# A 16-piece, 64-byte DRAM-to-DRAM copy at the head of ScalarE's DMA queue, in a softmax with relative-position bias

## The chip, the cores and the metric

The kernel runs on one core of a Trainium2 (trn2) chip; nothing else runs on the chip's other cores as far as this case tells. The metric is device time in microseconds, the median of several executions. The profile comes from one execution of its own, whose time stands beside its span below.

## The reference

For each of 2 x 8 (batch, head) pairs there is a 2112 x 2112 matrix of float32 logits. A bias that depends only on the clipped distance between row and column is added, and a softmax is taken along each row:

```python
B, H, S = (2, 8, 2112)
max_rel = 16
rel = pos[:, None] - pos[None, :]
rel_clipped = np.clip(rel, -max_rel, max_rel) + max_rel
bias = rel_bias[:, rel_clipped].copy()          # rel_bias: (H, 33)
logits = logits + bias[None, :, :, :]
logits = logits - logits.max(axis=-1, keepdims=True)
exp = np.exp(logits)
return (exp / exp.sum(axis=-1, keepdims=True)).astype(np.float32)
```

Input and output are 285.5 MB each, and both must cross between DRAM and the on-chip memory once.

## The kernel before

The 2 x 8 x 2112 rows are one long list, cut into 128 equal runs of ROWS = 264 rows, one run for each partition. So 8 neighbouring partitions (PB = 8) hold one (batch, head) matrix, and there are 16 such groups. A tile takes R = 6 rows of every partition: 128 x 12672 float32, 6.49 MB (6336 KB). There are N = 44 tiles, and NBUF = 4 buffers X[0] to X[3] through which they turn in place.

For each tile: SyncE's queue (SP) loads it (`load`, L80). VectorE (DVE) takes each of the six rows, adds the bias from a strip F and forms the negated row maximum (`add`, L187). ScalarE (ACT) takes exp with the row sum (`exps`, L196). DVE forms reciprocals of three rows at a time and scales the rows (`scale`, L204 and L208). ScalarE's queue stores the tile to the output (`store`, L84) once six rows are scaled. SP issues the load into a buffer again when the buffer's store has landed (the loop at L229). Everything is ordered by hand with semaphores: `take` waits for a count and takes it off again.

What comes ahead of the first tile matters here. SP issues load 0 at once, then a small load of 15 pieces of 10,240 bytes into the last buffer (L110, 150 KB; load 3 overwrites it later), then loads 1 and 2, and load 3 when the small one has landed. ScalarE's queue waits until DVE has cleared 264 columns of F (L99), then loads rel_bias into F, one row of 1,056 bytes for each of the 16 groups (L102). DVE waits for that (L143), turns it into the long bias line M in PSUM (L143 to L176), copies a strip of M into F (L181), and starts on tile 0 (L187). ScalarE's next work after L102 is the exp of tile 0, with its table load (L196), and its next DMA is the first store (L84).

The last tile's store is issued in two halves. At the end SP waits for both.

Of the kernel before, what the change touches and what calls it, by code (L numbers as in the profile page):

```python
# [15 lines left out]
def kernel(  # L16
# [6 lines left out]
    nc = tc.nc  # L23
    P = 128
    B, H, S, S2 = logits.shape
# [3 lines left out]
    ROWS = B * H * S // P  # L29
    PB = S // ROWS  # L30
# [8 lines left out]
    FW = S + STEP - 1  # L39
    BIG = 3.0e38  # L40
    LOW, PAD = 32, 2560

    io = ctx.enter_context(tc.tile_pool(name="io", bufs=1))
    X = [io.tile([P, R * S], FP32, tag=f"X{b}", name=f"X{b}") for b in range(NBUF)]
# [9 lines left out]
    def view(t, offset, dims):  # L54

        return bass.AP(tensor=t.tensor, offset=t.offset + offset, ap=[[list(t.ap[0])[0], P]] + dims)

    def rows(t, j, n):

        return bass.AP(tensor=t.tensor, offset=t.offset + j * S, ap=[[ROWS * S, P], [1, n * S]])  # L60

    with tc.tile_critical(no_gpsimd_drain=True):  # L62
# [7 lines left out]
        idx = nc.alloc_semaphore("idx")  # L70
        dve = nc.alloc_semaphore("dve")
        even = nc.alloc_semaphore("even")
        landed = tc.alloc_semaphore("landed")

        def take(eng, sem, n):
            eng.wait_ge(sem, n).then_inc(sem, -n)  # L76


        def load(j, b):
            nc.sync.dma_start(out=X[b][:, :], in_=rows(logits, j, R)).then_inc(ld[b], 16)  # L80
# [11 lines left out]
        def then(ins):  # L92
            done[0] += 1
            ins.then_inc(dve, 1)

        def settle():
            v.wait_ge(dve, done[0])

        then(v.memset(F[:, 0 : H * W], 0.0))  # L99

        nc.scalar.wait_ge(dve, 1)
        nc.scalar.dma_start(  # L102
            out=bass.AP(tensor=F.tensor, offset=F.offset, ap=[[PB * list(F.ap[0])[0], P // PB], [1, H * W]]),
            in_=bass.AP(
                tensor=rel_bias.tensor, offset=rel_bias.offset, ap=[[0, P // PB], [1, H * W]]
            ),
        ).then_inc(rb, 16)
        load(0, 0)
        pad = X[NBUF - 1]
        nc.sync.dma_start(  # L110
            out=bass.AP(tensor=pad.tensor, offset=pad.offset + LOW * list(pad.ap[0])[0],
                        ap=[[4 * list(pad.ap[0])[0], 15], [1, PAD]]),
            in_=bass.AP(tensor=logits.tensor, offset=logits.offset + (LOW * ROWS + (NBUF - 1) * R) * S,
                        ap=[[4 * ROWS * S, 15], [1, PAD]]),
# [24 lines left out]
        for m, op in ((eq, ALU.is_equal), (gt, ALU.is_gt), (le, ALU.is_le), (lt, ALU.is_lt)):  # L139
# [4 lines left out]
            out=view(F, 0, [[W, H], [1, W]]), in0=view(F, 0, [[W, H], [1, W]]),  # L144
# [8 lines left out]
                           in_=view(F, RT, [[Q, 2], [PB, Q // PB], [0, PB]])))  # L153
# [9 lines left out]
            out=view(F, 0, [[W, PB], [1, W]]), in0=view(F, SC + 2 * PB, [[1, PB], [0, W]]),  # L163
# [7 lines left out]
            out=view(M, U, [[ROWS, PB], [1, W]]), in0=view(F, 0, [[W, PB], [1, W]]),  # L171
            in1=view(F, SC + 8 * PB, [[1, PB], [0, W]]), op=ALU.add))
        then(v.tensor_copy(out=view(M, U + W, [[ROWS, PB], [1, ROWS - W]]),  # L173
                           in_=view(F, SC + 7 * PB, [[1, PB], [0, ROWS - W]])))
# [91 lines left out]
```

## Time and profile before

| what | value |
|---|---|
| device time, median of 3 runs | 1328.96 us (1327.49 to 1329.62) |
| the profiled execution's own time | 1327.58 us |
| its span, first to last instruction | 1325.7 us |
| bytes moved by DMA in the span | 571.14 MB, mean 431 GB/s |
| VectorE busy | 977.9 us, 74% |
| ScalarE busy | 574.3 us, 43% |
| loads of a tile | 44, median 40.9 us from issue to landing |
| stores of a tile | 43 whole and 2 halves, median 56.4 us for a whole one |

The profiled execution lies 1.38 us under the median, inside the range of the three runs, and 1.88 us of its time lie outside the span. In the DMA part of the page, q1 is the queue that SP issues to and q10 is ScalarE's; q14 fetches instructions. A queue's share is the time that its packets took as a share of 16 DMA engines for the stretch asked about. A packet counts in the window in which it starts, so a share can come out a little over 1. A tile's DMA is 128 packets of 50,688 bytes, 8 on each of the 16 DMA engines, and one 4-byte semaphore packet on each engine. "DVEq" and "ACTq" stand for the engine's own instruction queue: a wait put down to line L76 (`take`) is a wait for a semaphore that was taken there, on DVE in `add` for a load, on ACT in `exps` for a row from DVE.

### The profile page before, as it was taken

The page shows a single profiled execution, that of the slowest core. Times are in us where ns is not written, and L with a number is a line of the kernel's source. Part 1 is how long each engine was busy: PE and PEld are TensorE (multiplying, and loading weights), DVE is VectorE, ACT ScalarE, POOL GpSimd, SP SyncE. Part 2 cuts the span into 40 slices and gives each one's busy share as a digit, 9 for nine tenths or more (in the row PEclk, how much of TensorE's full clock was granted, in tenths as well). Part 3 has the DMA queues.
Part 4 walks back from the last instruction along what each step waited for, and adds up shares of the span by engine and source line. Part 5 has one row for each costly group of instructions (what it writes and reads, how often), then busy time and mean ns, then how long its engine had stood idle before and what let it go on. Part 6 is the DMA issues. An engine that isn't in the chain of part 4 may idle for free. (4 is left out here: it accounts for less than half of the span.)

```text
span 1325.7 us, 2475 instructions
## 1 busy us (share of the span) xinstructions
DVE 977.9 (74%) x917; ACT 574.3 (43%) x538; POOL 0.4 (0%) x6
## 2 busy tenths in 40 slices
DVE  7998777667877787677778777766877787676774
ACT  3464333434444443334444443433444443333442
POOL 0000000000000000000000000000000000000000
DMA  9999999999999999999999999999999999999998
GB/s 409 419 425 440 437 424 434 440 436 422 437 439 436 425 436 439 428 430 439 440 424 433 440 437 424 436 440 431 428 437 440 425 431 440 439 422 436 439 436 355
DMA packets 12880, 571.14 MB, mean 431 GB/s; under 512 B 1455, under 2 KB 1471, under 8 KB 1471
## 3 DMA queue, kind: packets, MB, share of 16 engines
q1 hardware_dynamic: 6366, 285.63, 49.9%
q10 hardware_dynamic: 6512, 285.49, 49.8%
q14 instruction: 2, 0.02, 0.0%
HBM read 285.65 MB, written 285.47 MB: 431 GB/s over the span
## 5 line engine op out<-in xcount | busy, mean ns | idle before, releaser
L187 DVE CUSTOM_DVE_ANT_0 X<-X,F 128x2112 f32<-128x2112 f32 x264 | 605.2, 2355 | 307.5 <-DVEq L76 307.5
L196 ACT ACTIVATE X<-X,nmax 128x2112 f32<-128x2112 f32 x264 | 541.7, 2052 | 558.4 <-ACTq L76 538.3
L208 DVE TENSOR_SCALAR X<-X,rec 128x2112 f32<-128x2112 f32 x264 | 332.5, 1316 | 13.2
L196 ACT ACT_TABLE_LOAD x10 | 12.8, 1283 | 169.0 <-ACTq L76 169.0
L196 ACT ACTIVATION_READ_ACCUMULATOR X<-X,nmax 128x1 f32 x264 | 49.2, 186 | 0.0
L181 DVE COPY F<-M 128x2135 f32 x11 | 26.1, 2375 | 0.5 <-DVEq L210 0.5
L187 DVE DVE_READ_ACCUMULATOR2_ANT nmax<- 128x1 f32 x264 | 22.0, 83 | 0.0
L204 DVE RECIPROCAL rec<-tot 128x3 f32<-128x3 f32 x88 | 15.0, 171 | 0.0
L143 DVE TENSOR_TENSOR F<-F 128x264 f32<-128x264 f32 x1 | 0.4, 434 | 7.0 <-DMA F<-in_rel_bias_dram 7.0
L173 DVE COPY M<-F 128x1848 f32<-128x1848 f32 x1 | 2.1, 2079 | 0.0
L99 DVE MEMSET F<- 128x264 f32 x1 | 0.3, 278 | 1.1 <-SPq L62 1.1
L147 DVE TENSOR_REDUCE F<-F 128x33 f32<-128x264 f32 x1 | 0.6, 611 | 0.0
L170 DVE TENSOR_TENSOR M<-F 128x264 f32<-128x264 f32 x1 | 0.4, 442 | 0.0
L162 DVE TENSOR_TENSOR F<-F,rbS 128x264 f32<-128x264 f32 x1 | 0.4, 427 | 0.0
L140 DVE TENSOR_SCALAR F<-F 128x8 f32<-128x8 f32 x4 | 0.4, 168 | 0.0
L175 DVE COPY M<-rbS 128x247 f32<-128x247 f32 x1 | 0.4, 408 | 0.0
L150 DVE STREAM_TRANSPOSE F<-F 128x64 f32<-128x64 f32 x1 | 0.2, 245 | 0.0
L155 DVE STREAM_TRANSPOSE F<-F 128x64 f32<-128x64 f32 x1 | 0.2, 245 | 0.0
L160 DVE TENSOR_SCALAR F<-F,rbS 128x8 f32<-128x8 f32 x1 | 0.2, 231 | 0.0
L166 DVE SCALAR_TENSOR_TENSOR F<-F,rbS 128x8 f32<-128x8 f32 x1 | 0.2, 229 | 0.0
L161 DVE TENSOR_SCALAR F<-F,rbS 128x8 f32<-128x8 f32 x1 | 0.2, 225 | 0.0
L167 DVE SCALAR_TENSOR_TENSOR F<-F,rbS 128x8 f32<-128x8 f32 x1 | 0.2, 222 | 0.0
(15 smaller groups left out, 2.1 us busy)
## 6 DMA issues: line engine op xcount, KB each, us to landing
X<-in_logits_dram SPq DMA_DIRECT2D x44, 6336.0 KB, 40.9
out_dram<-X ACTq DMA_DIRECT2D x43, 6336.0 KB, 56.4
out_dram<-X ACTq DMA_DIRECT2D x2, 3168.0 KB, 15.5
X<-in_logits_dram SPq DMA_DIRECT2D x1, 150.0 KB, 17.5
F<-in_rel_bias_dram ACTq DMA_DIRECT2D x1, 16.5 KB, 8.1
```

The source lines that it names most:

```text
L140: then(v.tensor_scalar(out=m, in0=dp, scalar1=0.0, scalar2=None, op0=op))
L143: then(v.tensor_tensor(out=view(F, 0, [[W, H], [1, W]]), in0=view(F, 0, [[W, H], [1, W]]), in1=view(F, SC + 3 * PB, [[1, H], [0, W]]), op= ...
L147: then(v.tensor_reduce(out=F[:, RB : RB + W], in_=view(F, 0, [[1, W], [W, H]]), axis=mybir.AxisListType.X, op=ALU.add))
L162: then(v.tensor_tensor(out=view(F, 0, [[W, PB], [1, W]]), in0=view(F, SC + 2 * PB, [[1, PB], [0, W]]), in1=view(rbS, W - 1, [[0, PB], [-1, ...
L170: then(v.tensor_tensor(out=view(M, U, [[ROWS, PB], [1, W]]), in0=view(F, 0, [[W, PB], [1, W]]), in1=view(F, SC + 8 * PB, [[1, PB], [0, W]] ...
L173: then(v.tensor_copy(out=view(M, U + W, [[ROWS, PB], [1, ROWS - W]]), in_=view(F, SC + 7 * PB, [[1, PB], [0, ROWS - W]])))
L175: then(v.tensor_copy(out=M[:, 0:U], in_=low.to_broadcast([P, U])))
L181: v.tensor_copy(out=F[:, :], in_=M[:, bass.ds(ROWS - STEP - j, FW)]).then_inc(dve, 1)
L187: v.tensor_tensor_reduce(out=x, in0=x, in1=F[:, STEP - 1 - r : STEP - 1 - r + S], scale=-1.0, scalar=BIG, op0=ALU.add, op1=ALU.min, accum_ ...
L196: nc.scalar.activation(out=x, in_=x, func=EXP, scale=-1.0, bias=nmax[:, r : r + 1], accum_out=tot[:, r : r + 1],).then_inc(expd, 1)
L204: v.reciprocal(out=rec[:, r0 : r0 + HALF], in_=tot[:, r0 : r0 + HALF]).then_inc(inv, 1)
L208: v.tensor_scalar_mul(out=x, in0=x, scalar1=rec[:, r : r + 1]).then_inc(scaled, 1)
```

## The change

ScalarE's queue gets one DMA ahead of everything else. It copies 16 pieces of 16 float32 (64 bytes) from the logits straight to the output, DRAM to DRAM. Piece i is the start of matrix i, which is the start of partition 8i's run, at the same place in both tensors. The bytes written are no result; the first store writes the right ones over them. The DMA has a semaphore of its own, `seen`, and ScalarE takes its 16 counts after it has issued the load of rel_bias, so that no store can be issued ahead of its landing. The rest of the program is as before.

```diff
+    MARK = 16
...
+        seen = nc.alloc_semaphore("seen")
...
         then(v.memset(F[:, 0 : H * W], 0.0))
 
+        def marks(t):
+
+            return bass.AP(tensor=t.tensor, offset=t.offset, ap=[[PB * ROWS * S, P // PB], [1, MARK]])
+
+        nc.scalar.dma_start(out=marks(out), in_=marks(logits)).then_inc(seen, 16)
         nc.scalar.wait_ge(dve, 1)
         nc.scalar.dma_start(
...
         ).then_inc(rb, 16)
+        take(nc.scalar, seen, 16)
         load(0, 0)
```

ScalarE's instructions from the start of the program to its first exps stand so before the change; L102 is the load of rel_bias, L99 and L217 are jumps into the block and the loop, and X_58 is the first buffer.

```order
L261 UNCONDITIONAL_BRANCH [waits barrier_Pool_Activation_PE_DVE_SP_release]
L261 UNCONDITIONAL_BRANCH [waits SP_sequencer_49]
L102 DMA F<-in_rel_bias_dram 16x264 [waits dve]
L99 UNCONDITIONAL_BRANCH
L217 UNCONDITIONAL_BRANCH
L196 ACT_TABLE_LOAD [waits added]
L196 ACTIVATE X_58,tot<-X_58,nmax 128x2112
```

The same stretch with the change; lines have moved down by 5 to 8, so L109 is the load of rel_bias and L107 the new copy.

```order
L269 UNCONDITIONAL_BRANCH [waits barrier_Pool_Activation_PE_DVE_SP_release]
L269 UNCONDITIONAL_BRANCH [waits SP_sequencer_49]
L107 DMA out_dram<-in_logits_dram 16x16
L109 DMA F<-in_rel_bias_dram 16x264 [waits dve]
L101 UNCONDITIONAL_BRANCH [waits seen]
L225 UNCONDITIONAL_BRANCH
L204 ACT_TABLE_LOAD [waits added]
L204 ACTIVATE X_58,tot<-X_58,nmax 128x2112
```

The new copy stands ahead of the wait for `dve`, so it is issued without waiting for anything on DVE. The wait for `seen` stands between the load of rel_bias and the first wait for a row of tile 0. No instruction of DVE, POOL or SP has moved.

## The prediction

> **What bounds the kernel now.** I read the page first, for the busy shares.
>
> ```profile
> span 1325.7 us, 2475 instructions
> DVE 977.9 (74%) x917; ACT 574.3 (43%) x538; POOL 0.4 (0%) x6
> DMA  9999999999999999999999999999999999999998
> q1 hardware_dynamic: 6366, 285.63, 49.9%
> q10 hardware_dynamic: 6512, 285.49, 49.8%
> ```
>
> No engine is full, but the DMA line is at 90% or more in 39 of 40 slices, and the two queues together fill 49.9 + 49.8 = 99.7% of the 16 DMA engines' time. The list of waits says the same from the other side:
>
> ```profile
> DVE X L187 <- DVEq L76: 307.5, 42, 9.0
> ACT X L196 <- ACTq L76: 538.3, 44, 17.2
> ```
>
> DVE waits at 42 tiles, 307.5 / 42 = 7.3 us each, for a load to land. So compute has 7 us of slack a tile, and the time is the DMA engines' work plus whatever time they lose. I then asked for the DMA share and rate in stretches (the last two columns).
>
> ```profile
> core 0: us, DVE busy (x) ACT busy (x) POOL busy (x), PEclk, DMA share, GB/s
> 22.00:38.83 16.83, 16.53 (x17) 13.16 (x13) 0.00 (x0) 1.00 1.00 434
> ...
> 42.37:44.24 1.87, 1.87 (x3) 0.99 (x1) 0.00 (x0) 1.00 1.13 434
> 44.15:47.10 2.95, 2.95 (x3) 2.83 (x3) 0.00 (x0) 1.00 1.00 275
> 47.10:48.97 1.87, 1.87 (x3) 1.74 (x3) 0.00 (x0) 1.00 1.03 434
> 48.97:50.84 1.87, 1.87 (x3) 1.74 (x3) 0.00 (x0) 1.00 1.00 434
> ...
> 600.00:630.00 30.00, 21.48 (x21) 13.62 (x13) 0.00 (x0) 1.00 1.00 431
> ```
>
> The steady rate is about 434 GB/s with loads alone (22 to 38.83) and with loads and stores mixed (from 47.10). 434 GB/s over 1.87 us is 0.81 MB, sixteen packets of 50,688 bytes: each DMA engine moves one tile packet in 1.87 us. The odd stretch is 44.15 to 47.10: the engines are full by their share, and yet they move only 275 x 2.95 = 811 KB, again sixteen packets. That round took 2.95 us instead of 1.87. **1.08 us are lost on all 16 DMA engines at once**, and the queues tell when:
>
> ```profile
> q1 hardware_dynamic: 15, 0.76, 95.9%
> q10 hardware_dynamic: 1, 0.05, 4.0%
> ```
>
> Those are the packets that start in 44.15 to 47.10: fifteen of loads and one of the first store. The next window (47.10 to 48.97) has them the other way round:
>
> ```profile
> q10 hardware_dynamic: 15, 0.76, 93.9%
> q1 hardware_dynamic: 1, 0.05, 9.1%
> ```
>
> So the long round is the one just ahead of the first store's first packets, and one engine had taken its store packet a round earlier. The first store is issued at 41.11 (quoted below). Later changes between load and store cost nothing: 47.10 to 50.84 runs at 434.
>
> Two more losses stand at the ends. At the start:
>
> ```profile
> q1 hardware_dynamic: 32, 1.62, 102.8%
> ```
>
> These are the 32 load packets that start in 1.9 to 6.2. They took 1.028 x 4.3 = 4.42 us an engine, where two rounds would be 3.74: 0.68 us of first-packet latency. At the end:
>
> ```profile
> 1318.00:1320.00 2.00, 0.00 (x0) 0.00 (x0) 0.00 (x0) 1.00 0.94 406
> 1320.00:1321.00 1.00, 0.00 (x0) 0.00 (x0) 0.00 (x0) 1.00 0.18 76
> 1321.00:1322.00 1.00, 0.00 (x0) 0.00 (x0) 0.00 (x0) 1.00 0.18 76
> 1322.00:1323.00 1.00, 0.00 (x0) 0.00 (x0) 0.00 (x0) 1.00 0.12 51
> 1323.00:1324.00 1.00, 0.00 (x0) 0.00 (x0) 0.00 (x0) 1.00 0.12 51
> 1324.00:1325.70 1.70, 0.00 (x0) 0.00 (x0) 0.00 (x0) 1.00 0.00 0
> ```
>
> From 1320 on, 76 KB a microsecond are three packets of a half store (3168 KB / 128 = 24.75 KiB each). Thirteen engines are done at about 1320; two or three laggards work on until 1324, some 4 us longer. **The end is the slowest DMA engine's end.**
>
> **The change, part by part.** The rows of the start that it touches:
>
> ```profile
> 0.96 0.39 SPq L80 DMA_DIRECT2D X<-in_logits_dram  x1
> 1.09 0.28 DVE L99 MEMSET F<- 128x264 f32 x1 [1.09 <-SPq L62]
> 1.40 0.60 ACTq L102 DMA_DIRECT2D F<-in_rel_bias_dram  x1
> 9.47 0.43 DVE L143 TENSOR_TENSOR F<-F 128x264 f32<-128x264 f32 x1 [7.00 <-DMA F<-in_rel_bias_dram]
> 19.06 2.36 DVE L187 CUSTOM_DVE_ANT_0 X<-X,F 128x2112 f32<-128x2112 f32 x1 [0.66 <-DVEq L76]
> 21.54 1.28 ACT L196 ACT_TABLE_LOAD   x1 [21.54 <-ACTq L76]
> 41.11 0.38 ACTq L84 DMA_DIRECT2D out_dram<-X  x1
> ```
>
> *The issue.* One more DMA on ScalarE's queue, 0.38 to 0.60 us by its neighbours. It can start where SP's first did, at 0.96, and ends between 1.34 and 1.56, while rel_bias was issued at 1.40. So rel_bias is issued at most 0.16 us later.
>
> *The packets.* One of 64 bytes and one semaphore packet on each engine. The nearest rows are rel_bias's: its data in 6.2 to 8.2, its semaphores in 8.2 to 10.2.
>
> ```profile
> q1 hardware_dynamic: 16, 0.81, 95.1%
> q10 hardware_dynamic: 16, 0.02, 2.9%
> ...
> q10 hardware_dynamic: 16, 0.00, 0.5%
> ```
>
> 2.9% and 0.5% of 2 us are 0.06 + 0.01 = 0.07 us an engine. That is the low price of the new packets; I take 0.1. The high price is that the first write to the output costs the 1.08 us here that it costs at 44 us now; that case is weighed among the rivals.
>
> *The delay of rel_bias.* Its data packets started two load rounds after the loads began, and its semaphores one round later: ScalarE's queue got one packet for each load packet. With two more packets ahead of it, rel_bias lands 0 to 2 rounds later, 0 to 3.74 us. DVE's start at 9.47 moves by that, and tile 0's first row (19.06, with 0.66 us of waiting for load 0 ahead of it) by 0 to 3.1 us, and so the first store. Price to the end: nothing. Loads keep the engines full meanwhile: loads 0 to 3 are 4 x 6.49 = 26 MB, 60 us at 434 GB/s, so the queue has work until about 62 us, and the store at 41.11 has some 20 us of room before a gap opens. A store that comes later lets the loads run ahead by as much. If that cover were gone, the price would be the delay itself, up to 3.1 us.
>
> *The wait for `seen`.* Queued behind it on ScalarE are only the table load and tile 0's exps, which wait for DVE until 21.54. rel_bias, issued later, landed within 9.47. Price 0, unless the copy took over 20 us.
>
> *The stall at 44 us.* The copy makes each DMA engine write to the output once, at the start, so whatever the first write to it costs is paid there. The trace does not show what the 1.08 us consist of. Bounds: nothing is saved (the stall belongs to reading a tile out of the on-chip memory, or to any first change from load to store), or all 1.08. The nearest row is the one at 44.15 itself: it occurs once, on all engines, at the first store and at no later one, which is what a first-time cost looks like, while a cost of turning from load to store would return at 48.97. I take all of it: -1.08.
>
> [...]
>
> **The sum.** -1.08 + 0.1 + 0 + 0 = -1.0 us. In the profiled execution that is 1327.58 to 1326.6. That execution lies 1.38 us under the median of the runs, so against the median: 1328.96 - 1.0 = **1328.0 us**. This is 0.07%, and the three runs spread over 2.1 us; 0.2% (2.66 us), about what a measurement of this kernel can tell from no change, is more than twice the sum.
>
> **The rivals.**
>
> *No gain* (the change doesn't do what it could): the stall is latency of something the copy doesn't touch, such as the read of a tile, and stays; or it is paid in full at the start instead, where nothing hides it because the load rounds run back to back from the start. For it: the store's packets differ from the copy's in source and size. Against it: the 0.68 us of start-up latency is there anyway and could cover part. Time: from 1328.96 + 0.1 = 1329.1 (stall moved or unaffected) to 1328.96 + 0.1 + 1.08 = 1330.1 (stall kept, and paid again). [...]
>
> *Faster, by the laggards.* The three late engines cost 4 us at the end, more than the stall. If the single engine that took its store a round early (the one q10 packet in 44.15 to 47.10), and so ran out of step with the others, lags because of that, an even first store removes the lag. Time: 1328.96 - 1.0 - 2 to 4 = 1324 to 1326. For it: the lag comes from a few engines, not from the bulk. Against it: there are three laggards and one early engine.
>
> *Slower, by the laggards.* The same mechanism with the other sign: the first store's issue moves against the load rounds (by 0 to 3.1 us, not a whole number of 1.87 us), so that more engines take it a round early, run out of step, and one lags further. Price: a second such lag on the slowest engine, +4 us, less 1.0: 1332. It decides from the point at which the slowest engine loses over 2.66 + 1.0 = 3.7 us more than now. Against it: nothing shows that being out of step costs time.
>
> **How the numbers follow.** Forecast (stall gone, hidden start): 0.34, 1326.8 to 1329.4 with the spread of the runs. No gain: 0.22, 1329.1 to 1330.1. Faster by laggards: 0.26. Slower by laggards: 0.18. The first two are both within 0.2%: 0.56. The predicted time is the likeliest case's, 1328.0; the range that takes in all but the ends of the last two is 1324.0 to 1331.8.
>
> **What would show it.** In the changed profile, the round that ends with the first store's packets should take 1.87 us at 434 GB/s, not 2.95; q10 should show 16 more data packets and 16 more semaphore packets ahead of rel_bias; L143's counterpart on DVE should start 0 to 3.74 us later than 9.47; ScalarE's table load should still wait for DVE, not for `seen`. The first 32 load packets would take over 4.42 us an engine if the stall has only moved. The windows after the first engines finish show the laggards: a tail of 4 us as now means the forecast or no gain, a tail under 2 us or over 7 us means one of the other two. A gap in the DMA share between 50 and 90 us would prove the cover for the delayed start wrong.

## The result, and the profile after

The changed kernel took **1337.04 us** (median of 9 runs, 1329.80 to 1342.44), the kernel before beside it 1328.80 us (9 runs, 1326.88 to 1333.69). The ratio is 1.0057, 95% interval 1.0036 to 1.0079; it weighs all runs and is not the quotient of the two medians, which is 1.0062. That is slower by about 7.6 us (8.2 us between the medians), outside the predicted range of 1324.0 to 1331.8. Seven of the nine runs took 1335.87 us or more. The profiled execution took 1331.70 us for a span of 1329.9 us, so it is one of the two quicker ones; its end can be compared with that of before (1327.58), 4.1 us later, but it does not show the whole median.

The page after, its shares and queues:

```profile
span 1329.9 us, 2477 instructions
DVE 977.7 (74%) x917; ACT 574.5 (43%) x538; POOL 0.4 (0%) x6
DMA  9999999999999999999999999999999999999997
q1 hardware_dynamic: 6366, 285.63, 49.9%
q10 hardware_dynamic: 6544, 285.50, 49.7%
```

The work is the same but for the 32 new packets of q10 (6544 against 6512: 16 of data and 16 semaphores). The DMA engines are as full as before (the two queues 49.9% and 49.7%, against 49.9% and 49.8%), so the time was lost while they were busy, or at the end.

The start, from the timeline after (start, length, engine, line, operation, and in brackets the idle time ahead with what ended it):

```profile
0.93 0.66 ACTq L107 DMA_DIRECT2D out_dram<-in_logits_dram  x1
...
1.62 0.59 ACTq L109 DMA_DIRECT2D F<-in_rel_bias_dram  x1
...
13.16 0.43 DVE L151 TENSOR_TENSOR F<-F 128x264 f32<-128x264 f32 x1 [10.70 <-DMA F<-in_rel_bias_dram]
22.41 2.36 DVE L195 CUSTOM_DVE_ANT_0 X<-X,F 128x2112 f32<-128x2112 f32 x1 [0.32 <-DVEq L78]
...
24.88 1.28 ACT L204 ACT_TABLE_LOAD   x1 [24.88 <-ACTq L78]
...
44.45 0.39 ACTq L86 DMA_DIRECT2D out_dram<-X  x1
```

rel_bias is issued 0.22 us later than before, yet VectorE starts on it 3.69 us later (13.16 against 9.47), and the first store goes out 3.34 us later (44.45 against 41.11). ScalarE's queue shows why. These are its packets in the windows 6.2 to 8.2, 8.2 to 10.2, 10.2 to 12 and 12 to 14:

```profile
q10 hardware_dynamic: 16, 0.00, 0.6%
```
```profile
q10 hardware_dynamic: 17, 0.00, 0.6%
```
```profile
q10 hardware_dynamic: 15, 0.02, 2.4%
```
```profile
q10 hardware_dynamic: 16, 0.00, 0.5%
```

First the copy's data, then its semaphores, then rel_bias's data (0.02 MB), then its semaphores. Between any two of them each DMA engine carries one load packet of 50,688 bytes (15 to 18 of q1 start in each window). So the two small packets cost ScalarE's queue two load rounds, 2 x 1.87 = 3.74 us, though they keep an engine busy for under a hundredth of that (11 ns for the 64 bytes and 9 ns for the semaphore, by the packet records).

The place of the stall, in windows after (us, engines' busy time, TensorE clock, DMA share, GB/s):

```profile
44.37:46.24 1.87, 1.87 (x1) 0.00 (x0) 0.00 (x0) 1.00 1.01 434
46.24:49.10 2.86, 2.86 (x5) 2.38 (x3) 0.00 (x0) 1.00 1.08 304
49.10:50.97 1.87, 1.87 (x3) 1.87 (x2) 0.00 (x0) 1.00 1.02 434
52.00:82.00 30.00, 29.55 (x29) 20.64 (x20) 0.00 (x0) 1.00 0.99 416
```

The stall is still there: a round of 2.86 us, after 2.95 before. And something new stands behind it. 52 to 82 us runs at 416 GB/s; the same window before:

```profile
52.00:82.00 30.00, 29.40 (x31) 17.30 (x18) 0.00 (x0) 1.00 1.00 433
```

The DMA share is 0.99 or 1.00 in both, so the packets themselves took longer. The queues after, in 49.10 to 50.97, tell which engines:

```profile
q10 hardware_dynamic: 11, 0.56, 68.8%
q1 hardware_dynamic: 11, 0.25, 33.3%
```

0.56 MB are eleven store packets, 0.25 MB five load packets (the other six are semaphores). Eleven engines take their first store packet; five take a load packet first. Before, one engine stood out of step with fifteen.

Last, the end. The two halves of the last store, and VectorE's start on the last tile, before and after:

```profile
1285.68 2.36 DVE L187 CUSTOM_DVE_ANT_0 X<-X,F 128x2112 f32<-128x2112 f32 x1 [8.12 <-DVEq L76]
...
1303.57 4.35 ACTq L84 DMA_DIRECT2D out_dram<-X  x2
```
```profile
1289.63 2.36 DVE L195 CUSTOM_DVE_ANT_0 X<-X,F 128x2112 f32<-128x2112 f32 x1 [8.13 <-DVEq L78]
...
1307.53 4.35 ACTq L86 DMA_DIRECT2D out_dram<-X  x2
```

and the windows around it, before and after:

```profile
1304.00:1308.00 4.00, 3.48 (x3) 0.00 (x0) 0.00 (x0) 1.00 0.77 329
...
1320.00:1324.00 4.00, 0.00 (x0) 0.00 (x0) 0.00 (x0) 1.00 0.15 63
1324.00:1328.00 4.00, 0.00 (x0) 0.00 (x0) 0.00 (x0) 1.00 0.00 0
```
```profile
1304.00:1308.00 4.00, 3.85 (x5) 1.67 (x2) 0.00 (x0) 1.00 0.38 165
...
1320.00:1324.00 4.00, 0.00 (x0) 0.00 (x0) 0.00 (x0) 1.00 0.81 348
1324.00:1328.00 4.00, 0.00 (x0) 0.00 (x0) 0.00 (x0) 1.00 0.26 114
```

Two candidates stand here side by side. From 1304 to 1308 the engines are more than half idle after the change: the last tile's load lands 3.95 us later, its store is issued 3.96 us later, and the engines that are on time run dry. And from 1324 on a few engines still work, at 114 GB/s. Only one of them can set the time; the last experiment tells which.

The trace also has a record of every packet: queue, start, length, size. It does not name the engine, but a packet that starts where another ends is on the same one, and each engine has to carry 8 load and 8 store packets of every tile, so the 16 chains can be put together. What is said below of single engines is worked out in this way and is no row of the profile. By these chains the engine that ends last ended at 1324.4 before and 1328.6 after. Behind the engine that was foremost at the same packet number, the last one was:

```
                  62 us   156   249   343   530   810   1184   1280
before             0.9    1.2   2.6   4.0   4.4   4.4   4.4    4.4 us
after              2.4    5.3   6.3   7.3   8.2   8.5   8.5    8.5 us
```

The five engines that took a load packet first lost 2.8 to 5.0 us each between 50 and 173 us, the other eleven 0.0 to 0.2. That is a loss of engines, while they are busy, and most of it early. (At the very end the latest engine after the change is only 5.1 us behind the first, because the ten engines that were on time had stood idle for some 3 us. The latest one never stood idle.)

### The profile page after: what moved, and what is told of

It reads as the page before. It is cut to its first block, busy times and chain, and to the rows that moved or that the text cites. A ratio compares the mean times of both kernels' runs of the same rounds, so it can differ in the third digit from the quotient of the medians.

```text
span 1329.9 us, 2477 instructions
## 1 busy us (share of the span) xinstructions
DVE 977.7 (74%) x917; ACT 574.5 (43%) x538; POOL 0.4 (0%) x6
## 3 DMA queue, kind: packets, MB, share of 16 engines
q1 hardware_dynamic: 6366, 285.63, 49.9%
q10 hardware_dynamic: 6544, 285.50, 49.7%
## 5 line engine op out<-in xcount | busy, mean ns | idle before, releaser
L216 DVE TENSOR_SCALAR X<-X,rec 128x2112 f32<-128x2112 f32 x264 | 332.4, 1315 | 13.2
L151 DVE TENSOR_TENSOR F<-F 128x264 f32<-128x264 f32 x1 | 0.4, 432 | 10.7 <-DMA F<-in_rel_bias_dram 10.7
```

Of the source, the lines that this page charges most:

```text
L151: then(v.tensor_tensor(out=view(F, 0, [[W, H], [1, W]]), in0=view(F, 0, [[W, H], [1, W]]), in1=view(F, SC + 3 * PB, [[1, H], [0, W]]), op= ...
L216: v.tensor_scalar_mul(out=x, in0=x, scalar1=rec[:, r : r + 1]).then_inc(scaled, 1)
```

## The experiments

**Three theories** stood at the outset. *The write*: the copy's early write to the output does it. *The delay*: the later rel_bias does it, by bringing engines out of step at the first store. *The work*: the extra DMA itself. A fourth was formed as the runs came in, and then a fifth; both are named where they start.

**1. The copy without the write.** The copy goes to an unused spot on the chip instead of the output; all else is as in the changed kernel.

```diff
+    spot = io.tile([P, MARK], FP32, tag="spot", name="spot")
...
-        nc.scalar.dma_start(out=marks(out), in_=marks(logits)).then_inc(seen, 16)
+        nc.scalar.dma_start(
+            out=bass.AP(tensor=spot.tensor, offset=spot.offset,
+                        ap=[[PB * list(spot.ap[0])[0], P // PB], [1, MARK]]),
+            in_=marks(logits)).then_inc(seen, 16)
```

> The changed kernel, but the sixteen pieces of 64 bytes go to an unused spot on the chip instead of to the output. Everything else, the wait for them and their place ahead of rel_bias, stays. Theory 1 (step): the copy only delays rel_bias by two load rounds, and so the first store by 3.3 us, 1.8 rounds of 1.87 us; this makes five DMA engines take their first store packet a round after the others, these lose time, and the end waits for the slowest. The target doesn't matter: ratio to before about 1.006, first store issued near 44.4 us, engines split at the first store. Theory 2 (write): the early write to the output itself costs. Then ratio 1.000. Theory 3 (plain delay): a later first store costs as such: 1.006.

Measured: 1336.49 us (6 runs, 1333.24 to 1336.75), ratio 1.006 [1.0041, 1.008]. The first store:

```profile
44.38 0.39 ACTq L87 DMA_DIRECT2D out_dram<-X  x1
```

As slow and as late as the changed kernel, with nothing written to the output ahead of time. The write is out.

**2. The copy behind rel_bias.** Same copy, same write, but issued after the load of rel_bias.

```diff
-        nc.scalar.dma_start(out=marks(out), in_=marks(logits)).then_inc(seen, 16)
         nc.scalar.wait_ge(dve, 1)
         nc.scalar.dma_start(
...
         ).then_inc(rb, 16)
+        nc.scalar.dma_start(out=marks(out), in_=marks(logits)).then_inc(seen, 16)
         take(nc.scalar, seen, 16)
```

> The changed kernel with the copy to the output issued behind the load of rel_bias instead of ahead of it, still waited for. rel_bias is then not delayed: VectorE's wait for it ends near 9.5 us, the first store is issued near 41.1 us. Theory 1 (step) and theory 3 (plain delay): ratio to before 1.000, within 0.003. Theory 2 (write): 1.006 as in the changed kernel.

Measured: 1327.77 us (12 runs, 1326.64 to 1337.68), ratio 1.0002 [0.9983, 1.0022].

```profile
9.68 0.43 DVE L151 TENSOR_TENSOR F<-F 128x264 f32<-128x264 f32 x1 [7.21 <-DMA F<-in_rel_bias_dram]
...
41.24 0.38 ACTq L86 DMA_DIRECT2D out_dram<-X  x1
```

The copy is in the program, rel_bias is not late (9.68 against 9.47), and the cost is gone from the median. The work of the copy is out too. Two of the 12 runs were nonetheless as long as those of the changed kernel, 1337.68 and the profiled one, 1336.84 us; the paragraph on drift below comes back to that one.

**3. The delay without the copy.** The kernel before, with three copies on VectorE that do nothing useful, about 3.5 us, in the preparation of M.

```diff
+        for _ in range(3):
+            then(v.tensor_copy(out=M[:, 2400 : 2400 + 1120], in_=high.to_broadcast([P, 1120])))
+            settle()
```

> The kernel before, without any copy, with three idle copies of 1120 columns on VectorE ahead of the first strip, about 3.7 us, to put the first store where it is in the changed kernel (44.4 us). Theory 1 (step): ratio 1.006, and several engines split at the first store. Theory 3 (plain delay): 1.006. Theory 2 (write): 1.000.

Measured: 1333.32 us (9 runs, 1330.1 to 1341.6), ratio 1.005 [1.0029, 1.0071].

```profile
44.56 0.39 ACTq L84 DMA_DIRECT2D out_dram<-X  x1
```

**The delay alone costs what the change costs**, within the intervals. What is left is how 3.5 us of delay at 44 us, under a queue full of loads, become 5 to 8 us at the end.

**4 to 8. The size of the delay.** The same three copies with 1245, 855 and 1446 columns, four with 1509, and the changed kernel with two copies of 1337. The next theory was that the delay counts against the load rounds: a whole number of them would bring the engines back into step. When that failed (3 x 1245), a theory of level packets took its place; the table below says what level means.

> As the kernel before it, but with some 0.4 us more (three idle copies of 1245 columns, about 4.1 us), which puts the first store a whole number of load rounds (3.74 us) after that of the kernel before. Theory 1 (step): the engines take their first store together again, ratio 1.000 to 1.002. Theory 3 (plain delay): at least 1.006, since the first store is later still. Theory 2 (write): 1.000.

> No copy; idle work on VectorE (three copies of 855 columns) so that the first store is issued near 43.75 us, 2.6 us later than before. New theory (level): an engine loses time where its packets of load 3 and of store 0 run level, the k-th of the one next to the k-th of the other, which are of the same partition; that happens to an engine that has had one packet of load 3 ahead of its first store packet. At 43.75 us every engine takes its first store packet ahead of load 3, so none is level: ratio 1.000, between 0.997 and 1.002, store and load packets at 434 GB/s from 50 to 80 us. Plain delay theory: 1.004, in line with 1.005 for 3.4 us.

> No copy; idle work of four copies of 1509 columns, first store near 47.5 us, 6.4 us later than before. Level theory: every engine has had two packets of load 3 by then, one packet apart, so none is level: ratio 1.000 to 1.002. Plain delay theory: at least 1.008.

> No copy; idle work of three copies of 1446 columns, first store near 45.6 us, 4.5 us later than before. Level theory: all 16 engines have had exactly one packet of load 3, all are level, and each loses 4 to 5 us between 50 and 85 us: ratio 1.004 to 1.006, with a rate clearly under 434 GB/s from 50 to 85 us. Plain delay theory: about 1.006, but at 434 GB/s there.

> The changed kernel with its copy, and two idle copies of 1337 columns on VectorE besides, which put the first store near 47.5 us instead of 44.4. Level theory: the engines are past the level place, and the changed kernel is cured by being delayed further: ratio to before 1.000 to 1.002 instead of 1.006. Plain delay theory: 1.009 or more.

Measured (the rate is that of the window 52 to 82 us; "level" is the number of engines that had taken exactly one packet of load 3 ahead of the first packet of store 0, by the chains):

| kernel | first store | level | 52 to 82 us | median (runs) | ratio, 95% interval |
|---|---|---|---|---|---|
| before | 41.11 | 0 | 433 GB/s | | |
| 3 x 855 | 43.72 | 0 | 433 | 1332.50 (6) | 1.0046 [1.0028, 1.0064] |
| copy to the chip | 44.38 | 2 | 429 | 1336.49 (6) | 1.006 [1.0041, 1.008] |
| the change | 44.45 | 5 | 416 | 1337.04 (9) | 1.0057 [1.0036, 1.0079] |
| 3 x 1120 | 44.56 | 9 | 399 | 1333.32 (9) | 1.005 [1.0029, 1.0071] |
| 3 x 1245 | 44.97 | 15 | 375 | 1333.47 (12) | 1.0055 [1.0031, 1.0078] |
| 3 x 1446 | 45.62 | 16 | 373 | 1337.06 (6) | 1.0076 [1.0049, 1.0102] |
| copy and 2 x 1337 | 47.47 | 0 | 433 | 1336.59 (5) | 1.0071 [1.0058, 1.0084] |
| 4 x 1509 | 48.17 | 0 | 433 | 1332.82 (12) | 1.0032 [1.0012, 1.0053] |

The windows for none, nine and sixteen level engines (3 x 855, 3 x 1120, 3 x 1446):

```profile
52.00:82.00 30.00, 29.55 (x30) 19.79 (x20) 0.00 (x0) 1.00 1.00 433
```
```profile
52.00:82.00 30.00, 29.55 (x29) 20.64 (x20) 0.00 (x0) 1.00 0.99 399
```
```profile
52.00:82.00 30.00, 29.55 (x30) 20.55 (x21) 0.00 (x0) 1.00 0.98 373
```

Two things follow. First, the rate falls with the number of level engines, from 433 to 373 GB/s, at a full DMA share. An engine is level when its k-th packet of load 3 stands next to its k-th packet of store 0. Both DMAs are 128 packets of 50,688 bytes, one for each partition, 8 on each engine; that the two k-th packets are of the same partition, one in buffer X[3] and one in X[0], is the author's estimate from that, since no packet record names a partition. By the chains the packets of a level engine took 0.18 to 0.38 us longer than 1.87 us on average in 50 to 80 us, those of the other engines of this table 0 to 0.09 us longer. Second, **this is not the whole cost**. Three kernels with no level engine and the full 433 GB/s are slower as well; the expectation that they would come back to 1.000 failed for 3 x 855 and for the copy with a delay, and for 4 x 1509 (1.0032, expected at most 1.002) the interval leaves it open. The cost does not simply grow with the delay either: by that theory 4 x 1509 should have come to 1.008 or more and the copy with a delay to 1.009 or more, and both intervals end below. The kernel of 4 x 1509 split in two: five of its 12 runs at 1326.4 to 1327.9, six at 1335.9 to 1337.6. Neither the whole rounds nor the level packets by themselves explain the time.

The fourth theory came from the chains: **drift**. By it, an engine that has fallen behind goes on losing, whatever brought it there. In the copy with a delay, the last engine is 0.7 us behind at 62 us, 3.7 at 342, 8.1 at 623 and 13.8 at 1278. It does not lose evenly: 42 of its packets after 190 us, 0.08 to 0.92 us too long each, make up 10.7 us. Over 13 of the profiles here (before, after and experiments 1 to 8 and 13 to 15), from about 190 us on, for every engine and every 16 of its packets:

```
behind the foremost engine   windows   lost per 16 packets
under 1 us                     4045          10 ns
1 to 5 us                      2291          59 ns
5 to 9 us                       887         119 ns
9 to 12.5 us                    237         170 ns
over 12.5 us                     43          48 ns
```

The loss grows with the lag up to 12.5 us, and the lag stops at 13 to 14 us, about seven packets of 1.87 us (13.1 us): the copy to the chip reached 13.2 us at 717 us and still stood there at 1278. The table alone does not tell cause from effect, since an engine that is slow for another reason would be late as well; experiment 13 tries that.

No delay is needed for such a course. In the long profiled execution of experiment 2, with rel_bias in time and no engine level, the last engine is 0.9 us behind at 62 us, 5.1 at 623 and 13.5 at 1278. A delay makes the long course more frequent (two of 12 runs there, seven of nine of the changed kernel); it is not its only start.

**9. Lag without delay, first attempt.** Extra loads into X[3] on four neighbouring partitions, ahead of load 3.

```diff
+        for p0, cols in ((0, R * S), (4, R * S), (8, HALF * S)):
+            nc.sync.dma_start(
+                out=bass.AP(tensor=pad.tensor, offset=pad.offset + p0 * list(pad.ap[0])[0],
+                            ap=[[list(pad.ap[0])[0], 4], [1, cols]]),
...
```

> The kernel before with nothing delayed on VectorE or ScalarE and no copy, but with three small extra loads into the last buffer (overwritten by load 3 later) that only four of the 16 DMA engines carry: two tile packets and one half one, 4.7 us of work. These four engines are then as late as the five that fell behind in the changed kernel. Theory drift: an engine that is out of step with the others goes on losing, as it did in the traces so far (under 1 us late: 10 ns lost in 16 packets; 4 to 7 us late: 60 to 120 ns), so the four end 7 to 10 us late and the ratio is 1.003 to 1.006. Theory additive: late engines only stay late; the slowest engine of the kernel before ends 3.9 us late anyway, so 4.7 us cost at most 0.8 us: ratio 1.000 to 1.001.

Measured: 1351.09 us (6 runs, five of them 1346.40 to 1356.49, one 1527.91), ratio of the five 1.0172 [1.0138, 1.0206], but it is no test of drift. The window 20 to 40 us shows that more than four engines were held up:

```profile
20.00:40.00 20.00, 19.70 (x20) 13.62 (x13) 0.00 (x0) 1.00 0.84 233
```

Twelve engines at the pace of the kernel before (433 GB/s in that window) would have moved 433 x 12/16 = 325 GB/s. In 16 to 45 us there are two stretches of 4.35 us each (six slices of 0.725) in which no engine starts a packet of data (0 GB/s).

**10 to 12. Chip or DRAM.** On the kernel with 16 level engines, X[3]'s loads and X[0]'s stores were cut into two DMAs of 64 partitions, and then one side was swapped against the other; with a swap, the results of some tiles are not the reference's.

> The kernel whose 16 engines all ran level (idle work of three copies of 1446 columns), with the loads of the last buffer and the stores of the first each cut into two DMAs of 64 partitions, lower half first in both. Load 3 and store 0 still pass the same partitions, on the chip and in DRAM, at the same time. Control: 52 to 82 us should run near 373 GB/s, as uncut.

> As the control, but the first half of load 3 reads the lower half's rows from DRAM and puts them into the upper 64 partitions, and the second half the other way round (so the tiles of the last buffer are computed with the other half's rows). Load and store are level in DRAM rows, and apart in the partitions on the chip. If level loss is a matter of the rows in DRAM: near 373 GB/s from 52 to 82 us. If of the partitions on the chip: near 433.

> As the control, but the first half of load 3 reads the upper half's rows and puts them into the lower 64 partitions, and the second half the other way round (the tiles of the last buffer are computed with the other half's rows). Load and store are level in the partitions on the chip, and apart in DRAM rows. If level loss is a matter of the partitions on the chip: near 373 GB/s from 52 to 82 us. If of the rows in DRAM: near 433.

Measured, one run each: 1515.35, 1527.66 and 1581.43 us. The first of them is the control, without a swap:

```profile
52.00:82.00 30.00, 29.55 (x30) 20.55 (x20) 0.00 (x0) 1.00 1.03 330
```

The cut itself costs 14%, so these three tell nothing on their question. With the swaps the same window ran at 308 and 313 GB/s. Why DMAs of 64 partitions are slow is not shown.

**13. Lag without delay.** Extra loads into X[3] again, each on five partitions that lie four apart, meant as 2.5 packets (2.5 x 1.87 = 4.7 us) on each of five engines. q1 carries 30 packets more than before (6396 against 6366), 15 of data and 15 semaphores, so five of each for each of the three loads.

```diff
+        for p0, cols in ((0, R * S), (1, R * S), (2, HALF * S)):
+            nc.sync.dma_start(
+                out=bass.AP(tensor=pad.tensor, offset=pad.offset + (LOW + 1 + p0) * list(pad.ap[0])[0],
+                            ap=[[4 * list(pad.ap[0])[0], 5], [1, cols]]),
...
+            ).then_inc(late, 16)
```

> Before, with three small extra loads into X[3] that are carried by five of the 16 DMA engines only (two and a half packets, about 4.7 us of work on each of the five); load 3 waits for them and writes over them; no delay of rel_bias. It puts five engines about 4.7 us behind the other eleven at the start, and changes nothing else. Drift theory (an engine that is behind the others goes on losing, and the last engine sets the end): the five end 4.7 us plus what they lose on the way later than they do now, so a ratio of 1.003 to 1.006 (1333 to 1337 us), with the last windows showing five late engines. Rival (being behind costs nothing, the late engine's work is not even what counts because the loads of all engines wait for one another): the 4.7 us vanish or show as they are at the most, a ratio of 1.000 to 1.0035.

Measured: 1332.83 us (12 runs, 1330.88 to 1340.67), ratio 1.003 [1.0006, 1.0055], first store at 40.86 us, 435 GB/s in 52 to 82 us. The interval alone fits both sides. The chains decide: from 52 us on the five late engines lost 5.5 to 7.5 us more, of the other eleven nine lost 0.6 to 2.3 and two 4.5 to 4.6. In the profiled execution (1335.54 us) the last engine ended at 1332.3, where 4.7 us alone would have put it at about 1320.3 + 4.7 = 1325.0 (1320.3 being the end of an engine that loses nothing, as before). The engines on time stood idle for up to 10 us ahead of the last half stores, the first of which was issued at 1315.09, and ended at about 1331.1: the late engines had held up the last load for all. rel_bias and the first store were not delayed in this kernel. So **an engine that is late loses more**, though not only such engines do.

**14. Other rows of DRAM.** The kernel with 16 level engines, first load 3 reading rows 132 further.

```diff
-        load((NBUF - 1) * R, NBUF - 1)
+        nc.sync.dma_start(out=pad[:, :], in_=rows(logits, (NBUF - 1) * R + 132, R)).then_inc(ld[NBUF - 1], 16)
```

> The kernel with the delay of three copies of 1446 columns, but the first load 3 reads rows 132 further down each partition's run (so its tile's results are of other rows). Everything meets in time and on the same chip partitions as there, but the DRAM places that are read and written at the same moment lie elsewhere against each other. If the loss of level packets is made at the chip's partition, 52 to 82 us runs again at about 373 GB/s; if it is made by the distance of the DRAM addresses, at about 433.

```profile
52.00:82.00 30.00, 29.55 (x30) 20.55 (x21) 0.00 (x0) 1.00 0.99 387
```

387 GB/s (one run), near 373 and far from 433: with this other distance of the DRAM addresses level packets are nearly as slow. In experiment 9, by the chains, most engines had the k-th packets of a load and a store side by side that were two tiles apart, not three, and 52 to 82 us ran at 389 GB/s. What these kernels have in common, if load and store are dealt to the engines alike, is the chip's partition; that it is the place is the author's estimate, and no run shows it.

**15. Level undone: failed.** A small load on SP's queue ahead of load 3 was to shift load 3 by a packet.

```diff
+        nc.sync.dma_start(
+            out=bass.AP(tensor=spot.tensor, offset=spot.offset,
+                        ap=[[PB * list(spot.ap[0])[0], P // PB], [1, 16]]),
...
+        ).then_inc(even, 16)
```

> The kernel with the delay of three copies of 1446 columns, plus a load of 16 pieces of 64 bytes into an unused spot on the chip, on SP's queue just ahead of load 3: one packet more on each engine between load 2 and load 3, so that load 3's packets no longer stand level with the first store's while the first store is issued at the same time. Level theory: 52 to 82 us goes from 373 back to about 433 GB/s, and the ratio falls from 1.0076 to 1.004 to 1.005, what the delays without level packets gave. Rival (the lateness of the first store alone sets the time): the ratio stays near 1.0076 whatever the rate in 52 to 82.

It shifted nothing: 377 GB/s in 52 to 82 us, all 16 engines level. It was issued at 18.95 us, in the same queue as the loads, and ScalarE's queue has no DMA between rel_bias (issued at 1.40) and the first store; its packet took 11 ns, like the copy's, and cost no round. The run is in effect the 3 x 1446 kernel again, on another chip, at 1333.68 us (12 runs, 1330.68 to 1342.75), 1.0035 [1.0007, 1.0063], after 1.0076 [1.0049, 1.0102]; it shows how far such a ratio moves between two sets of runs.

**16 and 17. The last load in two halves.** A fifth theory: the delay is handed through to the end, where the last tile's late landing makes the other engines idle (165 GB/s in 1304 to 1308 us), and that wait sets the time. The last load was split so that VectorE could start on its first half, in the changed kernel and in the kernel before.

```diff
+                for sem, r0 in ((ld[b], 0), (even, HALF)):
+                    nc.sync.dma_start(out=X[b][:, r0 * S : (r0 + HALF) * S],
+                                      in_=rows(logits, ROWS - STEP + b * R + r0, HALF)).then_inc(sem, 16)
...
+        for sem, r0 in ((ld[NBUF - 1], 0), (even, HALF)):
+            add(NBUF - 1, sem, r0, HALF)
+            scale(NBUF - 1, r0, HALF)
```

> The changed kernel, with the last tile's load split into two loads of three rows each with semaphores of their own, so that VectorE begins the last tile when its first three rows have landed and the first half store can go some 7 us earlier. In the changed kernel ten of the 16 DMA engines run out of stores at about 1305.3 us and stand idle for 3 us until the first half store is issued at 1307.53. Laggard theory (the end is set by the late engines, which are never idle and whose lost time the wait for the last load does not touch): the idle stretch at 1304 to 1308 us goes, and the time stays that of the changed kernel, ratio 1.003 to 1.007 to before. Rival (the delay of the first store is handed through to the last load's landing, and the wait for it sets the end): the time falls by 3 us or more, ratio 1.000 to 1.003.

> The kernel before with the same split of the last load. Its engines run on to the half stores without a gap, so both theories expect no change: ratio 0.999 to 1.001. If the split itself costs or gains, it shows here.

Measured: 1337.09 us (5 runs), 1.0071 [1.0054, 1.0089], and 1329.85 us (12 runs), 1.0026 [1.0008, 1.0044]. The control was expected at 0.999 to 1.001 and came out above it, and the idle stretch did not go. The half store came later, not earlier (issued at 1317.33 and 1306.25, against 1307.53 and 1303.57). No verdict; the two against each other, 1337.09 / 1329.85 = 1.0054, repeat the change's cost.

**18. The last tile without its work.** The changed kernel, with tile 43 stored as it was loaded.

```diff
...
-                store(n * R, n % NBUF, 0, HALF, landed)
-                store(n * R, n % NBUF, HALF, R - HALF, landed)
+                take(nc.scalar, ld[n % NBUF], 16)
+                for s0 in (0, HALF):
+                    nc.scalar.dma_start(out=rows(out, n * R + s0, HALF),
+                                        in_=X[n % NBUF][:, s0 * S : (s0 + HALF) * S]).then_inc(landed, 16)
```

> The changed kernel with the last tile's work left out: tile 43 is loaded and stored as it is (no bias, no exp, no scaling), so its two half stores are issued as soon as its load has landed, 18 us earlier than in the changed kernel. No DMA engine can run out of stores then; the number and size of the packets are the same. Laggard theory (late engines, never idle, set the end): the stretch at 1304 to 1308 us fills up, the engines on time end some 3 us earlier, and the time stays that of the changed kernel: ratio 1.003 to 1.007. Rival (the wait for the last tile's landing and work sets the end): the time falls by 3 us or more from the changed kernel's, ratio 1.003 or less.

Measured: 1336.42 us (12 runs, 1330.02 to 1338.30), ratio 1.0055 [1.0038, 1.0072]. The issue of the two half stores and the windows of the profiled execution (1333.24 us):

```profile
1291.35 1.24 ACTq L241 DMA_DIRECT2D out_dram<-X  x2
```
```profile
1304.00:1308.00 4.00, 0.00 (x0) 0.00 (x0) 0.00 (x0) 1.00 0.87 374
...
1320.00:1324.00 4.00, 0.00 (x0) 0.00 (x0) 0.00 (x0) 1.00 0.31 133
1324.00:1328.00 4.00, 0.00 (x0) 0.00 (x0) 0.00 (x0) 1.00 0.12 51
1328.00:1332.00 4.00, 0.00 (x0) 0.00 (x0) 0.00 (x0) 1.00 0.03 13
```

The stores are issued 16 us earlier, 1304 to 1308 runs at 374 GB/s instead of 165, and most engines are done by about 1320.3, as in the kernel before. The time is as long as the changed kernel's all the same: 51 and then 13 GB/s are a few late engines and then a single one, which by the chains works to 1330.2. **The late engines set the time, not the wait for the last tile.** The chains of the other profiled executions, those of experiments 9 to 12 left aside, say the same: in none of them had the engine that ended last stood idle ahead of the last half stores, while in all but the kernel before and 3 x 855 engines on time had, for up to 13 us.

This also gives the numbers at which runs pile up. An engine that loses nothing ends at 1320.3; the time lies about 3.2 us above the end of the last engine (1327.58 - 1324.4, and 1333.24 - 1330.2 = 3.0). With no late engine that makes 1323.5 us. With a lag of seven packets it makes 1320.3 + 13.1 + 3.2 = 1336.6. Five of six runs with the copy to the chip lie at 1336.4 to 1336.8, all five with copy and delay at 1336.2 to 1336.6, and seven of the 120 runs of the kernel before at 1336.3 to 1338.5. Two of the nine runs of the changed kernel lie well above it (1340.89 and 1342.44 us); neither was profiled, and what they lost besides stays open.

## Why the prediction was wrong, point by point

- **What bounds the kernel**: right. The DMA engines are full until the last stores, and the slowest of them sets the end (experiment 18).
- **The issue**, at most 0.16 us: 0.22. **The packets**, 0.07 to 0.1 us: 0.6% twice, of 2 us, 0.02 us. **The wait for `seen`**, nothing: right; the table load at 24.88 waits for VectorE. None of them mattered.
- **The delay of rel_bias**, "Price to the end: nothing": **the step that failed.** Its length was right at its upper end, two rounds; the first store moved by 3.34 us, a little more than the 3.1 allowed for. Its cover, the loads that keep the engines full, held as well: no gap opened at 50 to 90 us, where the DMA share is 0.98 before and after. What failed is that a full engine was taken for an engine at full rate, and that engines were thought to run alike. The delay moved the first store against the load rounds. Five engines came to stand level, at 2.06 to 2.11 us a packet on average in 50 to 80 us instead of 1.87, fell 3 to 5 us behind, and some of them lost more as the run went on; the last of them is the end. Experiments 1 to 3 pin the cost on the delay: delay without write, 1.006; write without delay, 1.0002; delay alone, 1.005.
- **The stall at 44 us**, -1.08 taken in full: it measured 2.86 against 2.95 us, -0.09. The bound at which nothing is saved was the right one. Nothing of it moved to the start: the first 32 load packets took 1.044 x 4.3 = 4.49 us an engine, 4.42 before. What the long round consists of no run here shows.
- **The rivals.** *Slower, by the laggards* (0.18, 1332 us) is what happened, by the mechanism it names: the first store moves against the rounds, more engines are out of step, and one lags further. The sentence against it, "nothing shows that being out of step costs time", weighed too much: three late engines at the end were a loss in sight, and the chains would have shown how it grew from 0.9 to 4.4 us over the run. *Faster, by the laggards* did not come: in the kernel before, the engine that took its store a round early does end last by the chains (1324.4), but one that was in step ends at 1324.2. The price of *Slower, by the laggards*, one more such lag, +4 us, fits the profiled execution (4.2 us later) but not the median: by the chains of other runs a lag goes on to 13 us and more.
  The sign given for it, a tail of over 7 us, did not show in the windows: the tail is 5.1 us (1323.5 to 1328.6), since the late last load had held up the engines on time by some 3 us.
- **The range** took the dearest rival's price from the size of today's lag and added nothing for one that could grow.

What stays open: why level packets are slow (one other distance of the DRAM addresses changed little, 387 GB/s against 373; that it is the partition is an estimate that no run shows); why a late engine loses more, what starts it where nothing is delayed, and why it stops at about seven packets; and why a delay that leaves no engine level (3 x 855, 4 x 1509, copy and delay) still makes a long lag more frequent. None of the kernels tried is faster than the kernel before.

## What to carry to other kernels

Here, with the DMA engines full, a small DMA cost the one queued behind it on the same queue a full packet of the other queue for each of its packets, semaphores included (2 x 1.87 us for 64 bytes), so issue what is waited for first. This kernel ended with the latest of its 16 DMA engines (1328.6 us by the chains, 5.1 us behind the first), so in one that is bound by them read the tail and the lag of single engines, not the mean rate alone, and price whatever shifts loads against stores by how far one engine can fall behind. A DMA share near 1.00 says that engines are occupied, not that packets go at full speed (0.98 at 373 GB/s, 1.00 at 433): set the GB/s beside it.

## What the runs showed of the hardware that was not expected

- On a DMA engine whose load and store packets stood level, 50,688 bytes took 2.06 to 2.25 us on average in 50 to 80 us, instead of 1.87; with all 16 engines so, 373 GB/s instead of 433 (3 x 1446 against 3 x 855).
- Engines ran apart: in 13 profiles the loss of one grew with its lag, from 10 ns per 16 packets under 1 us to 170 ns at 9 to 12.5 us, and was smaller beyond (48 ns in 43 windows).
- DMAs of 64 partitions among full ones brought loads and stores to 308 to 330 GB/s in 52 to 82 us (experiments 10 to 12); with loads into four neighbouring partitions 20 to 40 us ran at 233 GB/s (experiment 9).
- The first store's long round, 2.95 us, was still 2.86 us when the output had been written to before.
